# The end of a hybrid encoder layer: the last 256 tokens of three w_down blocks computed with tokens on the output's partitions

## The chip, the core and the metric

The kernel runs on one core of a Trainium2 chip. A core has TensorE (PE, matrix products, with weight loads shown as PEld), VectorE (DVE), ScalarE (ACT), GpSimd (POOL), a queue engine (SP) and 16 DMA engines. Data lies in an on-chip memory of 128 partitions; products go to PSUM, eight banks of 128 x 512 float32. The metric is device time in microseconds (us), the median of the runs; lower is better.

## The reference, cut to what matters

One encoder layer on 512 tokens of width 1024, all in float32:

```python
x = x + 0.5 * swiglu(rms_norm(x, ffn1_norm), ...)     # (silu(h @ w_gate) * (h @ w_up)) @ w_down, inner width 2752
h = rms_norm(x, mix_norm); u = h @ w_in
x = x + concat([fourier_mixer(u), gqa_attention(u)]) @ w_out
x = x + 0.5 * swiglu(rms_norm(x, ffn2_norm), ...)
return rms_norm(x, final_norm)                         # x / sqrt(mean(x*x) + 1e-6) * final_norm
```

The change concerns the last two lines: the last part of the second feed-forward's w_down product, its addition to x with the factor 1/2, and the final norm.

## The kernel before, in words

**Layout.** x lies transposed: feature on the partition (eight blocks `x[0]` to `x[7]` of 128 features), token on the free axis. Every operand of a float32 product is split into a high and a low part, and `product` (lines 153 to 156) does three TensorE products, high x high, high x low and low x high, into one PSUM accumulation. Each has its own weight load of 128 columns from the stationary operand, while the moving operand streams 256 or 512 columns.

**Memory.** Tiles come from pools that are laid one behind the other in each partition: `const` (with `ring`, twelve slots of 4 KB that hold the split weights, then `gx` with gains and x, then small ones: sums, means, powers), `weights` (three raw tiles, tag `raw`), `temps`, and behind these a region used by stage: in a feed-forward `at` (split activations, the moving operand of w_down), `rt` (split inputs of the seven-product scheme) and `sums` (raw gate and up weights `raw_g`, `s`, `raw_u`). The function `room` (line 87) leaves a gap; `room(cp, 192)` stands behind `ring`, and two of 192 bytes ahead of `at` and of `rt` (lines 257 and 259). A small tile takes a multiple of 32 bytes. In the program as built `ring` starts at byte 8320 of a partition, `at` at 110464 and `rt` at 139328; in the mixing stage a tile `more` of further weights starts at 110464 as well.

**Feed-forward.** The inner width is done in four groups. The first group's gate and up products are plain; the others go through `seven` (line 411): Winograd-like, seven half-size products in place of eight. Its `multiply` (line 422) issues all of them at line 429:

```python
nc.tensor.matmul(
    ps[:, c], a[:, ks], b[:, i, c], start=first and i == 0 and o == 0,
```

with `a` a 128-column piece of a `ring` slot as weights and `b[:, i, c]` 256 columns of `rt` as the moving operand (in the first product of a group two of them are cut into 64 and 192 columns). After each group comes w_down, for the eight output blocks d = 0 to 7: `down` (line 560) converts a block's weights into two slots (line 146 the high part on ScalarE, line 117 the low part on VectorE), and its steps stream 512 columns of `at`. `residual` (line 580) adds half the PSUM bank to `x[d]`. Raw weights are loaded some blocks ahead, by SP (line 132).

**Order.** Feed-forward runs in the order in which it is written on PE and SP; from the second group on ScalarE and VectorE follow it too. GpSimd is left to the scheduler. The mixing stage follows a written list.

**The end.** In the last group (seven column blocks of the inner width) w_down runs in full for d = 0 to 4. For d = 5, 6, 7 `closing` (line 1402) first does tokens 0 to 255 (`t0`), 21 products of 256 columns a block, each followed by residual (VectorE), square (ScalarE), addition of the squares (line 1409) and multiplication by the final gain in place (`gained`, line 1393). Then it does the same for tokens 256 to 511 (`t1`); between those products PE sums the squares of the first 256 tokens over the partitions (line 209, a product with a column of ones), 1/rms goes through VectorE and GpSimd (`mean`, line 216, and `power`, line 223), is turned into a row by transposes (line 228) and `finish` (line 1377) multiplies and stores the first 256 tokens. Behind the last product the same chain runs for tokens 256 to 511, with `awake` products (line 1400) as fillers, and nine stores in all go to one output tensor `out_y`, feature on the partition; the host transposes it.

Of the kernel before, what the change touches and what calls it, by code (L numbers as in the profile page):

```python
# [6 lines left out]
F32 = mybir.dt.float32  # L7
# [6 lines left out]
P = 128  # L14
# [16 lines left out]
USES = "a11", "s1", "a12", "s2", "s4", "s3", "a22"  # L31
KH = KD // 2
HEAD = 64
HI_DVE = ("f0", "f1")
SWAP_DMA = ("q1", "q2", "q3")

# [38 lines left out]
def asf(ap):  # L75
    return ap.bitcast(F32)
# [3 lines left out]
def encoder(ctx, tc, A, out):  # L80
# [17 lines left out]
    def bank(name):  # L98
        return pp.tile([P, S], F32, tag="bank", name=name)
# [58 lines left out]
    class Norm:  # L158
# [71 lines left out]
        def row(self, c0=0, c1=4):  # L230
# [4 lines left out]
            t = slice(c0 * P, c1 * P)  # L235
            nc.scalar.copy(self.rb[:, t], ps[:, t])
            return ps

        def rows(self, c0, c1):

            pss = [bank(f"rp{self.n}_{c0}{i}") for i in range(2)]
            for ps in pss:
                for c in range(c0, c1):
                    self.turn(ps, c)
            t = slice(c0 * P, c1 * P)
            nc.scalar.copy(self.rb[:, t], pss[1][:, t])
            return pss[0]

    def ffn(norm, after, wgu, wd, wdt, groups, opening, closing):

# [5 lines left out]
        with tc.tile_pool(name=f"act{n_}", bufs=1) as ap, tc.tile_pool(name=f"sums{n_}", bufs=2) as sp:  # L256
# [329 lines left out]
            for gi, group in enumerate(groups):  # L586
                last = gi == len(groups) - 1
                ahead, waiting, downs = [], [], []

                def more_downs(n):  # L590
                    while len(downs) < min(n, KD):
                        downs.append(down(len(downs), group, gi))

                if gi:
                    with in_full_order():
                        rest = seven(
                            range(group[0] + 1, min(group[-1] + 2, NF)), *ready, lambda i: more_downs(i + 1)
                        )
                else:
                    lent = [at[:, i].rearrange("p a b -> p (a b)") for i in range(PLACES - 4, PLACES)]  # L600
                    plain.extend(lent)
                    row = []
                    pss = dict(enumerate(opening(gate, lambda: norm.column([norm.acc]), lambda: row.append(norm.row()))))
                    back(lent[:2])
                    due, parts, left = [*pss, "t"], list(range(KH)), range(2 * len(pss), 2 * n_plain)
                    pss["t"] = [gate(2 * NF)]
                    tail_weights()
                    for i, c in enumerate(left):
                        pss.setdefault(c // 2, []).append(gate(c, by_dma=i in (1,) if n_ else i > 0))
                        if due:  # L610
                            j = due.pop(0)
                            for _ in evacuate(at[:, place(j)], n_, pss[j], norm):
                                pass
                        if c % 2 and c != left[-1]:
                            due.append(c // 2)
                        while len(parts) * len(left) > (len(left) - 1 - i) * KH:
# [12 lines left out]
                with in_full_order():  # L629
                    for d in range(KD):  # L630
                        if last and closing and d == KD - 3:
                            break
                        if last and d == KD - 2:
                            back(lent)
                        ps = bank(f"dn{n_}_{d}_{gi}")
                        if not last and d in (0, 4):
                            new = Pair(groups[gi + 1][0] + 1 + d // 4)
                            new.load_rest()
                            if d == 0:
                                ready = [new]  # L640
                                ahead.extend(new.steps())
                            else:
                                ready.append(new)
                        steps = downs[d](ps, every)
                        for _ in range(len(group) - (last and d < 2)):
                            next(steps)
                        waiting.append((d, ps, steps))
                        if last and d == 0:
                            rest()
                            lent = slots[KD - 2 : KD]  # L650
                            plain[0:0] = lent
                            more_downs(3)
                            continue
                        for d_, ps, steps in waiting:
                            for _ in steps:
                                pass
                            residual(d_, ps, every)
                        more_downs(d + (3 if gi and not last else 4))
                        if not gi:
                            next(left_over, None)  # L660
                        elif d == 0:
                            rest()
                        for d_, *_ in waiting:
                            added(d_)
                        waiting = []
                if last and closing:
                    closing([(e, down(e, group, gi) if e >= len(downs) else downs[e]) for e in range(KD - 3, KD)], residual)
                if not gi:
                    back(lent)
                free.extend(where[j] for j in group)  # L670
# [706 lines left out]
    def finish(c0, c1, row, parts):  # L1377
# [3 lines left out]
        for ks in parts:  # L1381
# [5 lines left out]
                y = xt[:, block, t]  # L1387
                nc.vector.tensor_tensor(out=y, in0=y, in1=pr[:, t].unsqueeze(1).to_broadcast(list(y.shape)), op=ALU.mult)
            queue = nc.scalar if ks[0] in by_pool else nc.sync
            queue.dma_start(out=out[:, block, t], in_=xt[:, block, t])  # L1390

    def gained(k, t=slice(0, S)):
        nc.scalar.activation(x[k][:, t], x[k][:, t], AF.Copy, scale=gains[:, 3, k : k + 1])

    def awake(n):

        unit = ident.bitcast(BF16)
        ps = bank("awake")
        for _ in range(2 * n):
            nc.tensor.matmul(ps[:, : 2 * P], unit[:, :P], unit, start=True, stop=True)  # L1400

    def closing(downs, residual):

        for k in range(downs[0][0]):
            gained(k)
        t0, t1 = slice(0, S // 2), slice(S // 2, S)

        def more(sq, t):
            nc.vector.tensor_tensor(out=n3.acc[:, t], in0=n3.acc[:, t], in1=sq[:, t], op=ALU.add)

        for d, steps in downs:
            ps = bank(f"last{d}0")
            for _ in steps(ps, t0):
                pass
            residual(d, ps, t0)
            more(n3.square(d, t0), t0)
            gained(d, t0)
        i = 0
        for d, steps in downs:
            ps = bank(f"last{d}1")  # L1420
            for _ in steps(ps, t1):
                i += 1
                if i == 5:
                    n3.column([n3.acc], 0, 2)
                if i == 9:
                    finish(0, 2, n3.row, ((0, 1), (4, 5), (2, 3), (6, 7)))
            if d < KD - 1:
                residual(d, ps, t1)
                sq = n3.square(d, t1)
                if d == downs[0][0]:  # L1430
                    more(sq, t1)
                gained(d, t1)

        pc = bank("ss3_2")
        for c in (2, 3):
            n3.sum(pc, c, [n3.acc], first=c == 2, last=False, skip_group_check=True)
        awake(1)
        for c in (2, 3):
            n3.sum(pc, c, [sq], first=False, last=False, skip_group_check=True)
        residual(KD - 1, ps, t1)  # L1440
        sq = n3.square(KD - 1, t1)
        gained(KD - 1, t1)
        for c in (2, 3):
            n3.sum(pc, c, [sq], first=False, last=c == 3, skip_group_check=True)
        awake(2)
        n3.mean(pc, 2, 4)
        n3.power(2, 4)
        finish(2, 4, n3.rows, ((0,), (1,), (4, 5), (2, 3), (6, 7)))

    with in_order():  # L1450
        ffn(n2, n3, A["wgu2"], A["wd2"], A["wdt2"], GROUPS2, lambda gate, column, row: [[gate(0, {KD - 1: column}), gate(1, {3: row})]], closing)


def _order():
# [37 lines left out]
def _layout(i):  # L1492
# [13 lines left out]
    def down(w):  # L1506
# [29 lines left out]
        "wins": chunks(w_in[:, np.concatenate([k, q, v])]),  # L1536
        "winf": w_in[:, :512].reshape(2, 4, P, 2, 256).transpose(3, 0, 2, 1, 4).reshape(4, P, 4, 256),
        "wo": chunks(i["w_out"][mix]),
    }


# [19 lines left out]
```

## Time and profile before

| what | us |
|---|---|
| median of the runs | 843.41 |
| profiled execution | 843.26 |
| its span, first to last instruction | 841.0 |
| PE busy | 833.3 (99%) |
| PE weight loads busy | 754.4 (90%) |
| DVE busy | 606.1 (72%) |
| ACT busy | 463.5 (55%) |
| POOL busy | 63.5 (8%) |

"Busy" counts overlapping products once, so a busy PE says only that a product was under way. The chain that ended last follows the work back from the last instruction to what released it at each step. A group row gives line, engine, operation, output <- inputs, shape and count, then busy us, mean ns of one, and the idle time ahead of it. A window row gives the window, its length, then busy us and instructions of PE, PEld, DVE, ACT and POOL, the granted clock of PE, the busy share of the DMA engines and GB/s. In the chain and the timeline the first number is the start in us, the second the length.

### The profile page before, as it was taken

To read this page: it belongs to the slowest core of one execution; us is meant where nothing else is said; L and a number is where in the kernel's file an instruction comes from. 1 tells how busy PE (TensorE), PEld (TensorE's weight loads), DVE (VectorE), ACT (ScalarE), POOL (GpSimd) and SP (SyncE) were. 2 spreads that over 40 slices of the span, in tenths; PEclk is the share of its full clock that TensorE was granted. 3 is DMA by queue.
4 is the path that set the end of the run, shared out by engine and by line. 5 is a ranking of instruction groups with operands and counts; after the bars stand their busy time and mean duration, and the time that the engine had idled before them with its cause. 6 is when DMAs were issued, how large, how long until landed. Compare 5 with 4: busy or idle time off the path is not lost.

```text
span 841.0 us, 13697 instructions
## 1 busy us (share of the span) xinstructions
PE 833.3 (99%) x5440; PEld 754.4 (90%) x5440; DVE 606.1 (72%) x927; ACT 463.5 (55%) x771; POOL 63.5 (8%) x70
## 2 busy tenths in 40 slices
PE   9999999999999999999999999999999999999996
PEld 6888998899989998889988888899988998899986
DVE  6987884578557867699998478788755884578563
ACT  7753663366435644677776346456533663366452
POOL 0121000000000000222000000110000100000002
PEclk9999999999999999999999999999999999999998
DMA  7796774467365423414020325778563674556123
GB/s 250 188 225 163 195 188 142 123 164 215 104 161 148 122 60 110 150 51 139 27 74 26 98 57 146 190 191 211 161 175 101 177 206 134 121 160 184 45 66 100
DMA packets 46382, 116.76 MB, mean 139 GB/s; under 512 B 5232, under 2 KB 10864, under 8 KB 46192
## 3 DMA queue, kind: packets, MB, share of 16 engines
q1 hardware_dynamic: 38240, 92.05, 33.2%
q0 software_dynamic: 7536, 23.34, 16.7%
q8 instruction: 42, 0.69, 0.3%
q10 hardware_dynamic: 544, 0.52, 0.2%
q14 instruction: 20, 0.16, 0.1%
HBM read 111.44 MB, written 2.10 MB: 135 GB/s over the span
## 4 chain that ended last, share of the span: by engine, by line
PE 94%; DVE 3%; DMA 1%; issue 1%; ACT 0%; POOL 0%; POOLq 0%; SPq 0%; ACTq 0%
PE r L429 23%; PE q L429 11%; PE dn L156 8%; PE dn L154 8%; PE dn L155 8%; PE p L429 6%; PE mix L154 4%; PE mix L156 3%; PE mix L155 3%; PE gu L762 3%; PE mix L1252 2%; PE mix L1209 2%; PE gu L154 1%; PE gu L155 1%; PE gu L156 1%; DMA raw_dn<-in_wd 1%
## 5 line engine op out<-in xcount | busy, mean ns | idle before, releaser
L429 PE MATMUL r<-rt,ring 128*128 128x256 f32 x1686 | 204.9, 276 | 0.0
L429 PEld LDWEIGHTS r<-rt,ring 128*128 128x128 f32 x1686 | 198.5, 188 | 0.9
L155 PE MATMUL dn<-at,ring 128*128 128x512 f32 x295 | 114.8, 389 | 0.0
L156 PE MATMUL dn<-at,ring 128*128 128x512 f32 x295 | 114.8, 389 | 0.0
L154 PE MATMUL dn<-at,ring 128*128 128x512 f32 x295 | 114.8, 389 | 0.0
L429 PE MATMUL q<-rt,ring 128*128 128x256 f32 x840 | 106.6, 276 | 0.0
L374 ACT CAST ring<-s 128x1024 fp32r<-128x1024 f32 x70 | 73.5, 1050 | 58.0 <-DVE s L394 53.0
L581 DVE SCALAR_TENSOR_TENSOR gx<-dn,gx 128x512 f32<-128x512 f32 x61 | 42.1, 691 | 81.7 <-PE dn L156 81.7
L429 PEld LDWEIGHTS q<-rt,ring 128*128 128x128 f32 x840 | 100.4, 188 | 0.0
L146 ACT CAST ring<-raw_dn 128x768 fp32r<-128x768 f32 (+2 forms) x51 | 43.6, 858 | 80.4 <-PE dn L155 76.8
L117 DVE TENSOR_TENSOR ring<-s,ring 128x1024 fp32r<-128x1024 f32 x70 | 85.3, 1218 | 0.6 <-ACT ring L374 0.6
L156 PEld LDWEIGHTS dn<-at,ring 128*128 128x128 f32 x295 | 55.4, 188 | 11.5
L155 PEld LDWEIGHTS dn<-at,ring 128*128 128x128 f32 x295 | 55.4, 188 | 11.1
L154 PEld LDWEIGHTS dn<-at,ring 128*128 128x128 f32 x295 | 55.4, 188 | 11.0
L346 POOL DMA_DIRECT2D s<-in_wgu x35 | 30.1, 861 | 427.2 <-DMA s<-in_wgu 171.1
L117 DVE TENSOR_TENSOR ring<-raw_dn,ring 128x768 fp32r<-128x768 f32 (+2 forms) x51 | 50.0, 984 | 5.8 <-ACT ring L146 5.5
L429 PE MATMUL p<-rt,ring 128*128 128x256 f32 x420 | 53.3, 276 | 0.0
L429 PEld LDWEIGHTS p<-rt,ring 128*128 128x128 f32 x420 | 50.2, 188 | 0.0
L117 DVE TENSOR_TENSOR ring<-raw_g,ring 128x1024 fp32r<-128x1024 f32 x35 | 42.6, 1217 | 0.0
L117 DVE TENSOR_TENSOR at<-u,at 128x512 fp32r<-128x512 f32 x35 | 24.2, 693 | 20.3 <-ACT at L484 20.2
L472 DVE TENSOR_TENSOR u<-g,u 128x512 f32<-128x512 f32 x35 | 24.0, 686 | 19.8 <-ACT u L469 19.8
L374 ACT CAST ring<-raw_g 128x1024 fp32r<-128x1024 f32 x35 | 36.8, 1051 | 0.0
(308 smaller groups left out, 1551.3 us busy)
## 6 DMA issues: line engine op xcount, KB each, us to landing
s<-in_wgu SPq DMA_DIRECT2D x70, 256.0 KB, 4.3
s<-in_wgu POOLq DMA_DIRECT2D x35, 512.0 KB, 5.6
raw_g<-in_wgu SPq DMA_DIRECT2D x35, 512.0 KB, 4.2
raw_dn<-in_wd SPq DMA_DIRECT2D x44, 384.0 KB, 3.9
raw_u<-in_wgu SPq DMA_DIRECT2D x35, 256.0 KB, 4.5
raw_gu<-in_wgu SPq DMA_DIRECT2D x12, 512.0 KB, 3.5
raw_o<-in_wo SPq DMA_DIRECT2D x8, 512.0 KB, 3.5
raw_dn<-in_wd SPq DMA_DIRECT2D x8, 448.0 KB, 4.0
```

Of the source, the lines that this page charges most:

```text
L117: nc.vector.tensor_tensor(out=lo, in0=src, in1=asf(hi), op=ALU.subtract)
L146: nc.scalar.copy(hi[:, :n, :], raw[:, :n, :])
L154: nc.tensor.matmul(ps, whi, mhi, start=first, stop=False)
L155: nc.tensor.matmul(ps, whi, mlo, start=False, stop=False)
L156: nc.tensor.matmul(ps, wlo, mhi, start=False, stop=last)
L346: nc.gpsimd.dma_start(out=blocks(t), in_=up, accum_op=ALU.add)
L374: nc.scalar.copy(ts[0], src)
L429: nc.tensor.matmul(ps[:, c], a[:, ks], b[:, i, c], start=first and i == 0 and o == 0, stop=i == KH - 1 and o == 2, skip_group_check=not fi ...
L472: nc.vector.tensor_tensor(out=self["u"], in0=self["g"], in1=self["u"], op=ALU.mult)
L581: nc.vector.scalar_tensor_tensor(out=x[d][:, t], in0=ps[:, t], scalar=0.5, in1=x[d][:, t], op0=ALU.mult, op1=ALU.add)
L762: nc.tensor.matmul(pss[c], w[:, k % 2, c], m[k], start=k == 0 and m is hh and w is hi, stop=k == KD - 1 and w is lo,)
L1209: nc.tensor.transpose(pts[n][:, c * P : (c + 1) * P], prob[t, b, c][:, kc * P : (kc + 1) * P], ident)
```

## The change

Blocks 5, 6 and 7 of the last group keep the old way for tokens 0 to 255. For tokens 256 to 511, in two chunks of 128, the roles are exchanged: the activations (128 tokens) are the stationary operand, and the weights of all three blocks, 384 columns, the moving one, so the product comes out with tokens on the partitions. Its PSUM bank (`high`) is started with transposes of x[4] to x[7] for that chunk; the products are accumulated on the last 384 columns. To this end the three blocks' weights are halved in the conversion and lie side by side in six slots (0 to 2 the high parts, 3 to 5 the low ones), 64 bytes into them. x[0] to x[3], already multiplied by the gain, are transposed into a second bank (`low`). The squares of the 384 columns are summed along the free axis by ScalarE into a [128,1] tile (`ssend2`, `ssend3`, both new in the `const` pool) and added to the mean that the other five blocks gave; 1/rms is then a number per partition, and ScalarE and VectorE scale `low` and `high` into `y`, which takes a raw weights' place. The final gains of the upper four blocks come as a new input `fg` of 128 x 512. The output is two tensors: the first 256 tokens as before, the last 256 with tokens on the partition. `Norm.rows`, `awake` and `closing` go.

In the program as built every engine has the same instructions in the same order as before up to the conversion of block 5's weights. `at` now starts at byte 110528, `rt` at 139392, `more` at 110528; `ring` stays at 8320.

```diff
+    class Ending:
+        def __init__(self, at, where, js, wd):
...
+            self.w = [
+                ring[:, a : a + 3].rearrange("p s c -> p (s c)")[:, 16 : 16 + len(js) * ENDS * P].rearrange(
+                    "p (j d c) -> p j d c", d=ENDS, c=P
+                )
+                for a in (0, 3)
+            ]
+        def weights(self, d):
+            n, js = len(self.js), self.js
+            raw = raw_tile(self.wd[d][:, js[0] : js[-1] + 1, :], f"end{d}", n)[:, :n]
+            hi, lo = (w[:, :, d - self.first] for w in self.w)
+            nc.scalar.activation(hi, raw, AF.Copy, scale=0.5)
+            nc.vector.scalar_tensor_tensor(out=lo, in0=raw, scalar=0.5, in1=asf(hi), op0=ALU.mult, op1=ALU.subtract)
...
+        def by_columns(self, d, t):
+            ps = bank(f"last{d}0")
+            for i, j in enumerate(self.js):
+                whi, wlo = (w[:, i, d - self.first] for w in self.w)
+                product(ps[:, t], whi, wlo, *self.acts(j, t), i == 0, i == len(self.js) - 1)
...
+        def by_tokens(self, c, between={}):
+            t = slice(c * P, (c + 1) * P)
+            low, high = bank(f"low{c}"), bank(f"high{c}")
+            self.turned(high, range(KH, KD), t)
+            whi, wlo = (w.rearrange("p j d c -> p j (d c)") for w in self.w)
+            ps = high[:, S - ENDS * P :]
+            for i, j in enumerate(self.js):
+                between.get(i, int)()
+                if i == 3:
+                    self.turned(low, range(KH), t)
+                h, l = self.acts(j, t)
+                for a, w in ((h, whi), (h, wlo), (l, whi)):
+                    nc.tensor.matmul(
+                        ps, a, w[:, i], start=False, stop=i == len(self.js) - 1 and a is l, skip_group_check=True
+                    )
+            sq = tp.tile([P, S], F32, tag="sq", name=f"sqend{c}")
+            ss = cp.tile([P, 1], F32, name=f"ssend{c}")
+            nc.scalar.activation(sq[:, : ENDS * P], ps, AF.Square, scale=D**-0.5, accum_out=ss)
+            r = n3.r[:, c : c + 1]
+            ms = n3.ms[:, c : c + 1]
+            nc.vector.tensor_tensor(out=ms, in0=ms, in1=ss, op=ALU.add)
+            n3.power(c, c + 1)
+            y = wp.tile([P, D], F32, tag="raw", name=f"y{c}")
+            nc.scalar.activation(y[:, :S], low, AF.Copy, scale=r)
+            nc.vector.scalar_tensor_tensor(out=y[:, S:], in0=high, scalar=r, in1=self.gain, op0=ALU.mult, op1=ALU.mult)
+            for h in range(2):
+                cs = slice(h * S, (h + 1) * S)
+                nc.sync.dma_start(out=out[1][(c - 2) * P : (c - 1) * P, cs], in_=y[:, cs])
+        def run(self):
+            self.gain = tp.tile([P, S], F32, tag="g", name="gain")
+            nc.sync.dma_start(out=self.gain, in_=A["fg"])
...
+            for d in range(self.first, KD):
+                self.by_columns(d, t)
+                if d == self.first:
+                    for c in (2, 3):
+                        n3.sum(pc, c, [n3.acc], first=c == 2, last=c == 3, skip_group_check=True)
+                    n3.mean(pc, 2, 4)
+            self.by_tokens(2, {
+                2: lambda: n3.column([n3.acc], 0, 2),
+                6: lambda: finish(0, 2, n3.row, ((0, 1), (4, 5), (2, 3), (6, 7))),
+            })
+            self.by_tokens(3)
```

`by_columns` goes on with residual, square, addition and gain for its block as before, `turned` issues one transpose per block into a bank, and `more_downs` calls `ending.weights(d)` for d = 5, 6, 7.

More of the change, by code (lines that the diff above doesn't have):

```diff
@@ L33 @@
 HEAD = 64
+ENDS = 3
 HI_DVE = ("f0", "f1")
@@ L237, in row @@
             return ps
[L239 to L247, printed above, removed]
     def ffn(norm, after, wgu, wd, wdt, groups, opening, closing):
@@ L588, in ffn @@
                 ahead, waiting, downs = [], [], []
+                ending = closing(at, where, list(group), wd) if last and closing else None
                 def more_downs(n):
                     while len(downs) < min(n, KD):
-                        downs.append(down(len(downs), group, gi))
+                        d = len(downs)
+                        downs.append(ending.weights(d) if ending and d >= KD - ENDS else down(d, group, gi))
                 if gi:
@@ L630, in ffn @@
                     for d in range(KD):
-                        if last and closing and d == KD - 3:
+                        if ending and d == KD - ENDS:
                             break
@@ L665, in ffn @@
                         waiting = []
-                if last and closing:
-                    closing([(e, down(e, group, gi) if e >= len(downs) else downs[e]) for e in range(KD - 3, KD)], residual)
+                if ending:
+                    more_downs(KD)
+                    ending.run()
                 if not gi:
@@ L1389, in finish @@
             queue = nc.scalar if ks[0] in by_pool else nc.sync
-            queue.dma_start(out=out[:, block, t], in_=xt[:, block, t])
+            queue.dma_start(out=out[0][:, block, t], in_=xt[:, block, t])
     def gained(k, t=slice(0, S)):
         nc.scalar.activation(x[k][:, t], x[k][:, t], AF.Copy, scale=gains[:, 3, k : k + 1])
[L1395 to L1448, printed above, removed]
@@ new lines, in encoder, with acts, turned @@
+    class Ending:
+        def __init__(self, at, where, js, wd):
+            self.at, self.where, self.js, self.wd = at, where, js, wd
+            self.first = KD - ENDS
+            self.w = [
[10 more added lines that the diff above has]
+            nc.vector.scalar_tensor_tensor(out=lo, in0=raw, scalar=0.5, in1=asf(hi), op0=ALU.mult, op1=ALU.subtract)
+        def acts(self, j, t):
+            return (self.at[:, self.where[j], o, t] for o in range(2))
+        def by_columns(self, d, t):
[3 more added lines that the diff above has]
+                product(ps[:, t], whi, wlo, *self.acts(j, t), i == 0, i == len(self.js) - 1)
+            nc.vector.tensor_tensor(out=x[d][:, t], in0=ps[:, t], in1=x[d][:, t], op=ALU.add)
+            sq = n3.square(d, t)
+            nc.vector.tensor_tensor(out=n3.acc[:, t], in0=n3.acc[:, t], in1=sq[:, t], op=ALU.add)
+            gained(d, t)
+        def turned(self, ps, ks, t):
+            for i, k in enumerate(ks):
+                nc.tensor.matmul(
+                    ps[:, i * P : (i + 1) * P], x[k][:, t], ident, start=i == 0, stop=i == len(ks) - 1,
+                    is_transpose=True, skip_group_check=True,
+                )
[11 more added lines that the diff above has]
+                for a, w in ((h, whi), (h, wlo), (l, whi)):
+                    nc.tensor.matmul(
+                        ps, a, w[:, i], start=False, stop=i == len(self.js) - 1 and a is l, skip_group_check=True
+                    )
+            sq = tp.tile([P, S], F32, tag="sq", name=f"sqend{c}")
[14 more added lines that the diff above has]
+            nc.sync.dma_start(out=self.gain, in_=A["fg"])
+            for k in range(KH):
+                gained(k)
+            t = slice(0, 2 * P)
+            gained(KH, t)
+            pc = bank("ss3_2")
+            for d in range(self.first, KD):
[9 more added lines that the diff above has]
+            self.by_tokens(3)
@@ L1450, in encoder @@
     with in_order():
-        ffn(n2, n3, A["wgu2"], A["wd2"], A["wdt2"], GROUPS2, lambda gate, column, row: [[gate(0, {KD - 1: column}), gate(1, {3: row})]], closing)
+        ffn(n2, n3, A["wgu2"], A["wd2"], A["wdt2"], GROUPS2, lambda gate, column, row: [[gate(0, {KD - 1: column}), gate(1, {3: row})]], Ending)
 def _order():
@@ L1538, in _layout @@
         "wo": chunks(i["w_out"][mix]),
+        "fg": np.broadcast_to(i["final_norm"][KH * P :], (P, S)),
     }
@@ L1553 @@
     }
-    out = nc.dram_tensor("out_y", (P, KD, S), F32, kind="ExternalOutput").ap()
+    out = [
+        nc.dram_tensor(f"out_{n}", shape, F32, kind="ExternalOutput").ap()
+        for n, shape in (("cols", (P, KD, S // 2)), ("rows", (S // 2, D)))
+    ]
     with tile.TileContext(nc, schedule_with_timeline_sim=True) as tc:
@@ L1557 @@
     r = run_bass_kernel_spmd(nc, [{f"in_{n}": a for n, a in arrays.items()}], core_ids=[0])
-    y = np.asarray(r.results[0]["out_y"])
-    y = y.transpose(1, 0, 2).reshape(1, D, S).transpose(0, 2, 1)
+    cols, rows = (np.asarray(r.results[0][f"out_{n}"]) for n in ("cols", "rows"))
+    y = np.concatenate([cols.transpose(2, 1, 0).reshape(S // 2, D), rows])[None]
     return np.ascontiguousarray(y[:, np.argsort(_order())])
```

## The prediction

> **What bounds the kernel now.** I read the page first, then the chain that ended last, then short timelines.
>
> ```profile
> span 841.0 us, 13697 instructions
> PE 833.3 (99%) x5440; PEld 754.4 (90%) x5440; DVE 606.1 (72%) x927; ACT 463.5 (55%) x771; POOL 63.5 (8%) x70
> PE 94%; DVE 3%; DMA 1%; issue 1%; ACT 0%; POOL 0%; POOLq 0%; SPq 0%; ACTq 0%
> L429 PE MATMUL r<-rt,ring 128*128 128x256 f32 x1686 | 204.9, 276 | 0.0
> L429 PE MATMUL q<-rt,ring 128*128 128x256 f32 x840 | 106.6, 276 | 0.0
> L429 PE MATMUL p<-rt,ring 128*128 128x256 f32 x420 | 53.3, 276 | 0.0
> L156 PE MATMUL dn<-at,ring 128*128 128x512 f32 x295 | 114.8, 389 | 0.0
> ```
>
> TensorE is the bound: 94% of the chain, with no idle time ahead of its large groups. The largest is line 429, the seven-product scheme: 1686 + 840 + 420 = 2946 products; 12 of them are the narrower pieces of the first product of each of six groups, which leaves 2934 of 256 columns. Inside it nothing else is near the bound:
>
> ```profile
> 742.00:752.00 10.00, 10.00 (x90) 10.00 (x90) 8.29 (x13) 5.83 (x11) 0.00 (x0) 1.00 0.71 184
> ```
>
> Here PE and its weight loads are busy for all 10 us, VectorE for 8.3, ScalarE for 5.8, at full clock. A change of nanoseconds per product in this stage goes straight into the time. So I compared the spacing of products. First the chain, with start and length of each piece: 24 products of line 429, and 512-wide ones of w_down.
>
> ```profile
> 751.52 2.72 PE r L429 x24
> ...
> 801.90 0.23 PE dn L154
> 802.13 0.23 PE dn L155
> ...
> 810.74 0.23 PE dn L154
> ```
>
> Then the 256-wide products elsewhere: the window of the first half of the end (63 `last` products; two neighbours count in its x65), and the timeline in the middle of the kernel.
>
> ```profile
> 816.02:823.58 7.56, 7.56 (x65) 7.55 (x64) 4.09 (x7) 4.13 (x7) 0.00 (x0) 1.00 0.01 2
> ```
> ```profile
> 403.15 0.28 PE L1058 MATMUL mix<-ring 128*128 128x256 f32 x1
> 403.27 0.28 PE L1059 MATMUL mix<-ring 128*128 128x256 f32 x1
> 403.39 0.28 PE L1060 MATMUL mix<-ring 128*128 128x256 f32 x1
> ```
>
> Line 429 issues a 256-wide product every 2.72/24 = 113.3 ns. The end needs 7.56/63 = 120.0 ns for products of the same width, type and accumulation, and so does the projection in the middle (120 ns from row to row). The 512-wide ones are (810.74 - 801.90)/39 = 226.7 apart. Something makes line 429 6.7 ns faster, and the kernel's layout has one difference: where the moving operand lies against the stationary one. In the program as built, `ring`, which holds the weights, starts at byte 8320 of a partition (a multiple of 128) and all its pieces are multiples of 512 further on. `at` starts at 110464, also a multiple of 128; `rt` at 139328, 64 bytes past one. In the middle both operands lie in `ring`. So where both operands are in step modulo 128 bytes the spacing is 120, and where they are 64 apart it is 113.3.
>
> **The change part by part.**
>
> *The shift.* Up to the last group's third w_down block the built program has the same instructions in the same order on every engine, so one might cost everything before the end at nothing. But `ssend2` and `ssend3`, two [128,1] tiles in the `const` pool, take 32 bytes each, and everything allocated behind that pool moves by 64: `rt` to 139392, a multiple of 128; `at` to 110528, 64 past one. `ring` stays. Line 429 is now in step, the case that this trace shows at 120.0. Its cost: 2934 x (120.0 - 113.3) ns = 19.6 us, the upper bound. Nearest row below: just after an interruption in-step products start closer together, as in the first ones of the end:
>
> ```profile
> 816.02 0.28 PE L154 MATMUL last<-at,ring 128*128 128x256 f32 x1
> 816.13 0.28 PE L155 MATMUL last<-at,ring 128*128 128x256 f32 x1
> 816.25 0.28 PE L156 MATMUL last<-at,ring 128*128 128x256 f32 x1
> 816.37 0.28 PE L154 MATMUL last<-at,ring 128*128 128x256 f32 x1
> ```
>
> 0.11, then 0.12. Line 429 runs for hundreds of products without interruption, so I take nearly all: **+19.3**; lower bound nothing, if the layout isn't the reason. Nothing hides it, since PE has no idle time there.
>
> ```profile
> L1059 PE MATMUL mix<-more,ring 128*128 128x256 f32 x16 | 4.5, 282 | 0.0
> ```
>
> The other way round, this group and its neighbours of lines 1058 and 1060, 48 products whose moving operand lies in `more`, get faster by 6.7 ns, since `more` moves out of step with `ring`: **-0.3**.
>
> The 512-wide products also change step, by `at`. I take no change. The first `last` product above follows a 512-wide one, its operands are in step, a weight load runs beside it, and it still took 0.11: streaming 256 columns in step is possible in about 113 ns, so 512 at 227 is twice that, and what is slow at 256 is the weight load, for which 512 columns leave time. VectorE's conversions don't care for the step:
>
> ```profile
> L117 DVE TENSOR_TENSOR ring<-s,ring 128x1024 fp32r<-128x1024 f32 x70 | 85.3, 1218 | 0.6 <-ACT ring L374 0.6
> L117 DVE TENSOR_TENSOR ring<-raw_gu,ring 128x1024 fp32r<-128x1024 f32 x6 | 7.3, 1220 | 1.3 <-ACT ring L146 1.2
> ```
>
> `s` is 64 off `ring`, `raw_gu` in step: 1218 and 1220 ns.
>
> *The end on TensorE.* The timeline of before, and a group of transposes elsewhere in it:
>
> ```profile
> 401.92 1.04 PE L1209 MATMUL mix<-ident,e 128*128 128x128 f32 x8
> 402.72 0.36 PE L1058 MATMUL mix<-ring 128*128 128x256 f32 x1
> 402.92 0.28 PE L1059 MATMUL mix<-ring 128*128 128x256 f32 x1
> ...
> 817.98 0.69 DVE L193 TENSOR_TENSOR acc<-acc,sq 128x512 f32<-128x512 f32 x1
> ...
> 823.78 0.42 DVE L581 SCALAR_TENSOR_TENSOR gx<-last,gx 128x256 f32<-128x256 f32 x1 [1.19 <-PE last L156]
> 824.23 0.42 ACT L187 ACTIVATE sq<-gx 128x256 f32<-128x256 f32 x1 [1.56 <-DVE gx L581]
> 824.68 0.42 DVE L1409 TENSOR_TENSOR acc<-acc,sq 128x256 f32<-128x256 f32 x1 [0.48 <-ACT sq L187]
> ...
> 831.65 0.28 PE L156 MATMUL last<-at,ring 128*128 128x256 f32 x1
> 831.77 0.51 PE L209 MATMUL ss<-ones,acc 128*128 128x2 f32 x4
> ```
>
> From 816.02 to 831.77 are 15.75 us: 126 products at 0.120 are 15.12, and one pair of column sums and two turns of r the other 0.63, of which I give the sums two thirds, 0.42. After: 63 products stay, 7.56. The other 63 become 42 of 384 columns, at 384/256 of 113.3 or of 120 ns, 0.170 to 0.180 each; I take 0.172, 7.2 in place of 7.56: -0.34. Sixteen transposes come in four groups: in the rows eight take 0.80 and the product behind them 0.20 in place of 0.12, so a group of four is 0.44, four of them +1.76. The sums over tokens 256 to 511 come ahead of the last product: +0.42, and a wait. They need block 4's squares added, which VectorE had at 818.67 and now has 0.1 later (the last weights' low part becomes a scalar_tensor_tensor), while PE arrives at 816.02 + 21 x 0.12 = 818.54: +0.3. Together the last product starts 2.15 later, near 833.8, and its result is there at 834.15 (before: 831.93).
>
> Of the other waits put into PE's order, the sums over tokens 0 to 255 need residual, square and addition of the last block, 1.5 us by the three rows at 823.78; PE has a group of transposes and six products before them, 0.44 + 1.03. No cost, or a tenth. Their r has the following 2.4 us.
>
> *Behind the last product.* The timeline, then rows of grouped instructions, then of the DMA issues:
>
> ```profile
> 833.55 0.16 DVE L216 TENSOR_SCALAR ms<-ss 128x2 f32<-128x2 f32 x1 [1.15 <-PE ss L209]
> 833.78 0.70 POOL L223 TENSOR_TENSOR r<-ms,mhalf 128x2 f32<-128x2 f32 x1 [4.22 <-DVE ms L216]
> ...
> 837.12 0.39 ACTq L1390 DMA_DIRECT2D out_y<-gx  x1
> ```
> ```profile
> L1197 ACT ACTIVATION_READ_ACCUMULATOR e<-mix,mx,sc 128x1 f32 x32 | 6.3, 196 | 0.0
> ...
> L882 ACT ACTIVATE sq_q<-mix 128x512 f32<-128x512 f32 x4 | 2.4, 591 | 0.0
> ```
> ```profile
> L912 DVE SCALAR_TENSOR_TENSOR rot_q<-mix,qkg,cos 128x512 f32<-128x512 f32 x1 | 0.7, 749 | 0.4 <-ACT sw_q L895 0.4
> ```
> ```profile
> out_y<-gx SPq DMA_DIRECT2D x5, 256.0 KB, 2.4
> ...
> out_y<-gx ACTq DMA_DIRECT2D x2, 256.0 KB, 3.0
> ```
>
> Before, 5.2 us pass from the last product's result to the last issue at 837.12. Now: square of 384 columns out of PSUM 0.48 (from 0.591 for 512) and its accumulator 0.20, an addition 0.16, the power 0.70, then the two halves of y side by side, 0.75 on VectorE, with 0.05 between steps: 2.5, to 836.7. SP issues two transfers 0.39 apart, the last at 837.1: the same time as before. But 512 KB are on their way then, not 1 MB, since tokens 256 to 383 have left 4 us earlier, beside products. So the last transfer lands in 2.4 or a little less and not in 3.0: the end comes out **-0.5**. Bounds: -2 (transposes at the 0.06 that a quarter of a 512-wide product takes, no wait for VectorE) and +2 (products at 0.180, a microsecond more of waiting, landing in 3.0).
>
> Costed at nothing: the halved weights, 0.1 longer on VectorE per block under 4.8 us of products (21 x 0.227), into slots that are free since the last seven-product is over; without that cover 0.3. The gains' transfer on SP has nothing behind it until the first store.
>
> *The sum* is made against the profiled execution's 843.26 (span 841.0 and 2.3 around it), 0.15 below the median of 843.41: 843.26 + 19.3 - 0.3 - 0.5 = **861.8**.
>
> A rule speaks against this. The Trainium skill, "TensorE: Matmul & The Clock Gate", section "Step-by-step: what each phase is for", has two independent read ports, one for weights and one for the moving operand, so that loading the next weights doesn't take read bandwidth from the running product. By it the shift of 64 bytes costs nothing. The rows disagree with it so far: 113.3 and 120.0 ns for products that differ only in the step.
>
> Its section "PE-mode transpose" gives about 275 ns for a 128x128 transpose in a kernel. As an estimate by that page, sixteen would add 4.4 rather than 1.76. The trace has the 0.10 per transpose used above.
>
> **The rivals.**
>
> 1. *Not slower: the spacing has another cause than the addresses.* The seven-product stage writes other banks and runs beside more VectorE work than the end; if one of these sets the 6.7 ns, nothing before the end changes and the time is 843.26 - 0.5 = **842.8**. Against it: three groups in step, in two stages, all show 120, and busier neighbours should not make products faster. 11%.
> 2. *The 512-wide products gain what line 429 loses.* If being in step costs any product 6.7 ns, the 885 of w_down (3 lines x 295) come down from 226.7 to 220: 5.9 less, **855.9**, or 854 with the other 512-wide groups that change step. For it: 226.7 - 120.0 is 106.7, a clean rate. Against it: the 0.11 in step above. 13%.
> 3. *The end stalls*, on VectorE or on PSUM: its place is the accumulation of products on transposes in one bank, which no row shows. At 3 us or more, **865** and up. 6%.
>
> That the change doesn't do what it says is excluded by the built order of instructions, short of the results' values.
>
> **How the numbers follow.** The forecast, 861.8, has 70%; its own spread is about 860 to 864.5 (the end's bounds, and 18.5 to 19.6 for line 429). The range takes in rival 2, down to 853.5, and stops at 864.5; 842.8 and the long stall stay out. 2%, 17 us, is about what a measurement of this kernel can tell from no change, and 860.3 is that line: the forecast lies 1.5 above it, so a twentieth of its chance, rival 2 and rival 1 make 0.28 for within 2%; slower by more 0.71; faster 0.01.
>
> **What the profile after would show.** Chain pieces of 24 products of line 429 of 2.88 in place of 2.72, and their mean 283 in place of 276 (that is what `last` has now); w_down 512-wide unchanged at 0.227; about 19 us of the difference before the end begins; four groups of transposes of 0.44; from the last product's start to the span's end 6.7 in place of 9.4. I am wrong if line 429 stays at 2.72, or if w_down's spacing falls to 0.220.

## The result and the profile after

The kernel after takes **867.72 us** (median; 867.35 to 868.48) against 843.19 for the kernel before, measured beside it: 1.0294 times as long, 95% interval 1.0282 to 1.0306. It is slower, by 24.5 us, where 18.5 were forecast. One of the four executions of the kernel before took 2174.77 us, and the ratio leaves it out. The profiled execution took 867.68, its span is 865.5.

The page of the kernel after, engines and largest groups:

```profile
span 865.5 us, 13644 instructions
PE 858.7 (99%) x5417; PEld 773.8 (89%) x5417; DVE 603.9 (70%) x923; ACT 462.0 (53%) x770; POOL 62.5 (7%) x69
L420 PE MATMUL r<-rt,ring 128*128 128x256 f32 x1686 | 215.5, 283 | 0.0
L156 PE MATMUL dn<-at,ring 128*128 128x512 f32 x295 | 117.2, 397 | 0.0
L420 PE MATMUL q<-rt,ring 128*128 128x256 f32 x840 | 112.2, 283 | 0.0
```

TensorE still fills 99% of the span and nothing idles ahead of the large groups, but the mean of a seven-product multiplication (line 429 before, line 420 now) went from 276 to 283 ns, and that of a w_down product from 389 to 397. The second was to stay. The chain of the kernel after gives the spacing, 24 products of line 420, then 30 products of w_down of which the first and the last are shown:

```profile
763.84 2.88 PE r L420 x24
...
834.62 0.23 PE dn L155
...
841.39 0.23 PE dn L157
```

2.88/24 is 120.0 ns (113.3 before). (841.39 - 834.62)/29 is 233.4 ns (226.7 before). So *both* widths lost 6.7 ns, at most 2934 x 6.67 = 19.6 us for line 420 and 885 x 6.67 = 5.9 us for w_down. The timeline of the end:

```profile
841.45 0.27 PE L155 MATMUL last<-at,ring 128*128 128x256 f32 x1
...
849.59 0.60 PE L1426 MATMUL high<-ident,gx 128*128 128x128 f32 x4
849.94 1.29 PE L1444 MATMUL high<-ring,at 128*128 128x384 f32 x6
851.18 0.61 PE L210 MATMUL ss<-ones,acc 128*128 128x2 f32 x4
851.64 0.78 PE L1444 MATMUL high<-ring,at 128*128 128x384 f32 x3
...
857.42 2.33 PE L1444 MATMUL high<-ring,at 128*128 128x384 f32 x12
...
860.64 0.55 POOL L224 TENSOR_TENSOR r<-ms,mhalf 128x1 f32<-128x1 f32 x1 [2.95 <-DVE ms L1452]
861.23 0.75 DVE L1456 SCALAR_TENSOR_TENSOR y<-high,r,gain 128x512 f32<-128x512 f32 x1 [0.67 <-POOL r L224]
```

The end's first `last` product starts at 841.45, before at 816.02: 25.4 us are lost by then. Summed from each product's start to the next one's, in both traces, line 420 has 19.0 of them and w_down 5.6. Another 0.7 lie in the 120 gate and up products whose weights are a part of `at` (about 227 ns apart before, 233 after). Line 420 stays below 19.6 chiefly because 72 of its 2934 products stand between products of w_down; these were at 117.7 before and are at about 119.8 now. From there to the span's end it is 24.05 against 24.98: the new end is 0.9 us shorter.

### The profile page after: what moved, and what is told of

It is laid out like the page before. It is cut to its first block, busy times and chain, and to the rows that moved or that the text cites. A ratio compares the mean times of both kernels' runs of the same rounds, so it can differ in the third digit from the quotient of the medians.

```text
span 865.5 us, 13644 instructions
## 1 busy us (share of the span) xinstructions
PE 858.7 (99%) x5417; PEld 773.8 (89%) x5417; DVE 603.9 (70%) x923; ACT 462.0 (53%) x770; POOL 62.5 (7%) x69
## 4 chain that ended last, share of the span: by engine, by line
PE 98%; DVE 0%; issue 0%; ACT 0%; POOLq 0%; POOL 0%
PE r L420 23%; PE q L420 12%; PE dn L157 8%; PE dn L155 8%; PE dn L156 8%; PE p L420 6%; PE mix L155 3%; PE mix L156 3%; PE mix L157 3%; PE gu L757 3%; PE gu L155 3%; PE gu L156 3%; PE gu L157 3%; PE mix L1247 2%; PE mix L1204 2%; PE mix L1053 1%
## 5 line engine op out<-in xcount | busy, mean ns | idle before, releaser
L420 PE MATMUL r<-rt,ring 128*128 128x256 f32 x1686 | 215.5, 283 | 0.0
L420 PEld LDWEIGHTS r<-rt,ring 128*128 128x128 f32 x1686 | 208.9, 192 | 1.0
L156 PE MATMUL dn<-at,ring 128*128 128x512 f32 x295 | 117.2, 397 | 0.0
L155 PE MATMUL dn<-at,ring 128*128 128x512 f32 x295 | 117.1, 397 | 0.0
L157 PE MATMUL dn<-at,ring 128*128 128x512 f32 x295 | 117.1, 397 | 0.0
L420 PE MATMUL q<-rt,ring 128*128 128x256 f32 x840 | 112.2, 283 | 0.0
L420 PEld LDWEIGHTS q<-rt,ring 128*128 128x128 f32 x840 | 105.8, 192 | 0.0
L147 ACT CAST ring<-raw_dn 128x768 fp32r<-128x768 f32 (+2 forms) x48 | 40.6, 850 | 77.1 <-PE dn L156 73.7
L420 PE MATMUL p<-rt,ring 128*128 128x256 f32 x420 | 56.1, 283 | 0.0
L420 PEld LDWEIGHTS p<-rt,ring 128*128 128x128 f32 x420 | 52.9, 192 | 0.0
L118 DVE TENSOR_TENSOR ring<-raw_dn,ring 128x768 fp32r<-128x768 f32 (+2 forms) x48 | 46.7, 976 | 8.0 <-ACT ring L147 7.9
L452 DVE TENSOR_TENSOR g<-p,p 128x256 f32<-128x256 f32 x35 | 14.8, 424 | 39.1 <-PE p L420 39.1
```

What stands on the lines that cost most here:

```text
L118: nc.vector.tensor_tensor(out=lo, in0=src, in1=asf(hi), op=ALU.subtract)
L147: nc.scalar.copy(hi[:, :n, :], raw[:, :n, :])
L155: nc.tensor.matmul(ps, whi, mhi, start=first, stop=False)
L156: nc.tensor.matmul(ps, whi, mlo, start=False, stop=False)
L157: nc.tensor.matmul(ps, wlo, mhi, start=False, stop=last)
L420: nc.tensor.matmul(ps[:, c], a[:, ks], b[:, i, c], start=first and i == 0 and o == 0, stop=i == KH - 1 and o == 2, skip_group_check=not fi ...
```

## The experiments

All distances below are those of the moving operand from the stationary one, modulo 512 bytes. For line 420 that is `rt` against `ring`, for w_down `at` against `ring`. Before: `at` 256, `rt` 448. After: `at` 320, `rt` 0. The gaps (`room`) ahead of `at` and of `rt` set them freely.

**Before's addresses under the kernel after.**

```diff
-            room(ap, 192)
+            room(ap, 128)
             at = ap.tile([P, PLACES, 2, S], F32R, name=f"at{n_}")
```

> The changed kernel with the gap ahead of `at` cut from 192 to 128 bytes, so that `at` and `rt` lie where they lay before the change (110464 and 139328); the new end is kept. Theory addresses: line 420 goes from 120.0 back to 113.3 ns per product (19.5 us) and the 512-wide w_down products from 233.3 back to 226.7 (885 of them, 5.9 us), so 867.7 - 25.4 = about 842.3; against the kernel before what is left is the new end alone, about 1 us faster. Rival, the new end or its order slows what is ahead of it: stays near 867.

Measured: 842.87 against 843.08, ratio 0.9999, interval 0.9991 to 1.0008. The whole loss is gone, with the new end, its waits, its output and its tiles all in place. The microsecond that the new end was to gain doesn't show in the median. The page and the chain, a piece of the second group and one of the fourth:

```profile
L156 PE MATMUL dn<-at,ring 128*128 128x512 f32 x295 | 114.9, 389 | 0.0
L420 PE MATMUL r<-rt,ring 128*128 128x256 f32 x1686 | 206.1, 277 | 0.0
```
```profile
182.83 2.72 PE r L420 x24
...
572.32 2.83 PE r L420 x24
```

w_down is back at 389. Line 420 is at 113.3 in five of its six groups (three in each feed-forward); in the fourth it is at 2.83/24 = 117.9, with operands at the same distance. The fourth group costs 2.2 us by that (489 products x 4.4 ns). Two of the eleven executions, this profiled one (844.19) and another (844.74), lie 1.3 and 1.9 us above the median; for the second there is no trace to say whether it is the same.

**The shift alone**, under the kernel before: two tiles of 32 bytes that nothing uses.

```diff
     n3 = Norm(3)
+    for c in (2, 3):
+        nc.vector.memset(cp.tile([P, 1], F32, name=f"ssend{c}"), 0.0)
```

> The kernel before with two more [128,1] tiles in the const pool and nothing else (two memsets of 0.06 us): every tile behind the pool moves by 64 bytes as in the change, the end is the old one. Theory addresses: 843.2 + 19.5 + 5.9 and a few tenths = 868 to 869, slower than the changed kernel by the gain of its end (about 1 us). Rival, the change's own instructions cost the time: 843.

Measured: 868.84, ratio 1.0305 (1.0291 to 1.0319). So 64 bytes of unused memory make the kernel before as slow as the kernel after, and 1.1 us slower still: that is what the new end saves on these addresses (25.16 us from the first `last` product to the span's end in this trace, 24.09 in that of the kernel after).

**One operand at a time.** First `rt` moved to where it was before, `at` left at 320:

```diff
             at = ap.tile([P, PLACES, 2, S], F32R, name=f"at{n_}")
-            room(ap, 192)
+            room(ap, 128)
             rt = ap.tile([P, 7, 2, KH, HALF], F32R, name=f"rt{n_}")
```

> The changed kernel with the gap ahead of `rt` cut to 128 bytes: `rt` lies as before the change, `at` stays 64 bytes further up. Theory addresses, each operand by itself: line 420 at 113.3, w_down at 233.3, so about 867.7 - 19.5 = 848.2. Rival, the two are coupled (one bank pattern for the stage): another time, 842 or 867.

Measured: 854.00, ratio 1.0130 (1.0115 to 1.0146), span 851.6. The chain, a piece each of the first, the second and the fourth group:

```profile
98.80 2.72 PE r L420 x24
...
184.26 2.83 PE r L420 x24
...
577.82 2.72 PE r L420 x24
```

The first and the fourth group run at 113.3, the other four at 117.8, though `rt` lies where it was before. All six follow a w_down stage with `at` at 320. But ahead of the first and the fourth it is that of a plain group, whose last products have their weights in `at` as well, or in a tile that moved along, so that their distance stays a multiple of 256; they stand 226.7 apart. Ahead of the other four w_down comes to 229.0 ns by the starts in the trace, not to the 233.3 that it has after at the same distance. The time is neither the theory's 848.2 nor one of the rival's two, but the two terms aren't independent.

Then the reverse: `at` back at 256, `rt` left at 0.

```diff
-            room(ap, 192)
+            room(ap, 128)
             at = ap.tile([P, PLACES, 2, S], F32R, name=f"at{n_}")
-            room(ap, 192)
+            room(ap, 256)
             rt = ap.tile([P, 7, 2, KH, HALF], F32R, name=f"rt{n_}")
```

> The kernel after with gaps of 128 and 256 bytes: at 256 bytes from ring modulo 512 as in before, rt at 0 as in after. Theory (256-column products cost 120.0 at a distance that is a multiple of 256, 512-column ones 226.7 there and 6.7 more elsewhere, and the two terms add): w_down back at 226.7, line 420 at 120.0, so 19.6 more than the 839.4 to 840.5 of e10: a span of 859 to 860. Rival, the two terms are one, since w_down's rhythm goes over into the next group: then w_down or line 420 also lands elsewhere, as in e2, and the span is 2 us or more off that.

Measured: 861.51, ratio 1.0219 (1.0201 to 1.0237), span 859.2. The page, and the chain:

```profile
L420 PE MATMUL r<-rt,ring 128*128 128x256 f32 x1686 | 215.5, 283 | 0.0
L156 PE MATMUL dn<-at,ring 128*128 128x512 f32 x295 | 115.0, 390 | 0.0
```
```profile
186.79 2.88 PE r L420 x24
```

This is the case that the prediction described, line 420 at 120.0 and w_down unchanged, and its time lies by the 861.8 forecast for it. What the kernel after has above it, 865.5 - 859.2 = 6.3 us, is mostly `at`: by the starts in the two traces 5.2 in w_down (227.3 to 233.1 on average) and 0.7 in the gate and up products whose weights lie in `at`.

**Both operands elsewhere**, `at` at 448 and `rt` at 64, then `at` at 128 and `rt` at 384:

```diff
-            room(ap, 192)
+            room(ap, 320)
             at = ap.tile([P, PLACES, 2, S], F32R, name=f"at{n_}")
-            room(ap, 192)
+            room(ap, 128)
```

> The changed kernel with `at` 448 and `rt` 64 bytes past `ring` modulo 512 (before: 256 and 448; changed: 320 and 0). Theory parity, only the distance modulo 128 counts: line 420 at 113.3, w_down at 233.3, about 848. Theory direction, the distance modulo 256 counts and 64 ahead isn't 64 behind (the 256-wide products of the middle with their operand in `more` took 118 at 64 ahead): line 420 near 118, w_down unknown, about 860.

```diff
-            room(ap, 192)
+            room(ap, 0)
             at = ap.tile([P, PLACES, 2, S], F32R, name=f"at{n_}")
-            room(ap, 192)
+            room(ap, 256)
```

> The kernel after, with the gap ahead of at 0 and that ahead of rt 256 bytes: at 128 and rt 384 bytes from ring modulo 512, both multiples of 128. If the step modulo 128 decides: line 420 at 120.0 as in the kernel after, w_down back at 226.7, so 5.9 less than the kernel after, a span near 859.6. If the distance modulo 512 or 256 decides, line 420 at 384 may have 113.3 or 117.8 and the span lies between 840 and 853.

Measured: 859.03 with a span of 856.9, and 863.68 with 861.5. With `rt` at 64, line 420 was at 113.3 in the first group and at 117.8 in five; w_down at 448 was at 233.3. That is near the second theory's 860. In the second kernel, the chain in two groups:

```profile
94.06 2.85 PE r L420 x24
...
776.22 2.85 PE r L420 x24
```

118.7 at a distance of 384, and w_down at 128 came to 232.3 to 233.3 by the starts in the trace. Neither of the two numbers expected of this run came out: 128 is not like 0 and 256. The step modulo 128, on which the prediction rested, is not the rule.

**Products alone.** So the distance was swept in a kernel that computes nothing of the layer: 36 products in a row, three for each of four (256 columns) or seven (512) pieces of weights, in the order of the layer's, with all operands zero, on an otherwise idle core at full clock (granted clock 1.00); four such runs at each distance, behind one narrow product of 64, 96, 160 or 224 columns.

```python
for i in range(run // 3):
    ...
    for o, (a, b) in enumerate(((0, 0), (0, 1), (1, 0))):
        at = shift + a * D + k * P
        mv = d + (2 * k + b) * n
        nc.tensor.matmul(ps[:, :n], w[:, at : at + P], m[:, mv : mv + n], ...)
```

> A kernel of products alone (nothing of the layer is computed): runs of 36 products of 256 columns, then of 512, the moving operand 0, 32, ... 480 bytes from the stationary one modulo 512, four runs for each distance, behind one product of 64, 96, 160 or 224 columns. Theory A, the spacing goes by the distance modulo 128: 256 columns 120 ns at 0, 128, 256 and 384 and 113 at 64 and its like; 512 columns 226.7 at 0, 128, 256, 384 and 233.3 at 64 and its like, the same behind each of the four. Theory B, a distance allows several rhythms and the product ahead picks one: at 64 bytes some of the four runs at 113.3 and some at 117.8 for 256 columns, at 229 and at 233 for 512. Theory C, the addresses matter only beside the vector engines' traffic: one spacing for all, since no other engine works here.

Rows of its timeline: one row stands for consecutive products from the start given, so that its length less the last product's 0.28 (256 columns) or 0.39 (512), by the count less one, is the spacing. In order: 256 columns at 0, at 64 behind 64 columns, at 64 behind 96, then 512 columns at 0, 64 and 192.

```profile
30.05 3.88 PE L42 MATMUL bank<-m,w 128*128 128x256 f32 x31
...
65.51 3.11 PE L42 MATMUL bank<-m,w 128*128 128x256 f32 x26
...
69.74 3.22 PE L42 MATMUL bank<-m,w 128*128 128x256 f32 x26
...
311.17 5.83 PE L42 MATMUL bank<-m,w 128*128 128x512 f32 x25
...
378.37 5.89 PE L42 MATMUL bank<-m,w 128*128 128x512 f32 x25
...
514.05 6.00 PE L42 MATMUL bank<-m,w 128*128 128x512 f32 x25
```

These are about 120, 113, 118, 227, 229 and 234 ns, from rounded lengths. Mean spacing of the last 24 products of each run, by their starts in the trace (two values where the four runs differ); 256 to 480 bytes gave the same as 0 to 224:

| distance, bytes | 256 columns, ns | 512 columns, ns |
|---|---|---|
| 0 | 120.0 | 226.7 |
| 32 | 116.7 to 117.8 | 233.3 |
| 64 | 113.3 or 117.8 | 228.9 |
| 96 | 120.0 | 233.3 |
| 128 | 118.6 to 120.0 | 232.1 to 233.3 |
| 160 | 117.2 to 118.7 | 234.2 to 234.5 |
| 192 | 113.3 or 117.8 | 233.3 |
| 224 | 118.3 | 233.3 |

With the weights themselves moved by 64 bytes it was again the difference that counted: 120.0 and 226.7 with both operands moved, 113.3 or 117.8 and 233.3 with the weights alone. So it needs no traffic of the vector engines (theory C falls), the period is 256 and not 128 (A falls), and at 64 and 192 two spacings exist (B holds for 256 columns; the 512-column runs at 64 showed only one, while w_down in the layer showed 229.0 and 233.3 there). Which one a run takes depends on what goes ahead of it, but not on the narrow product's width alone: 113.3 came behind 64 columns at 64 and 192, and behind 96 and 224 columns with the weights moved. The run ahead and the PSUM banks changed along with it and weren't separated. The two widths want opposite things: 512 columns are fastest at 0, where 256 columns are slowest (with 96). Before's layout has `at` at 256, so 0, and `rt` at 448, so 192: the best of these distances for both, as long as line 420 takes the faster of its two spacings.

**How a group is entered.** In the layer the second product of each seven-product group is cut in two (`HEAD`). Two versions of the kernel after, with before's addresses and another cut each, and the kernel before with another cut (the first one's edit is shown, without the gap):

```diff
-HEAD = 64
+HEAD = 128
```

> The kernel after with before's addresses (gap of 128 bytes ahead of at), and the second product of each seven-product group cut into 128 and 128 columns in place of 64 and 192. Theory: which of the two rhythms, 113.3 or 117.8 ns, a group has at 448 bytes from ring is decided by how it is entered, so the cut changes the set of slow groups; the span is 839.9 plus 2.2 for each group of six at 117.8 (1.8 for the third), 840 to 853, with nothing else changed. Rival: the fourth group's 117.8 comes from what the mixing stage leaves behind; then it stays the fourth alone, and the span 842.1.

> As the one before, with the cut at 96 columns. Theory: again another set of slow groups or the same, 839.9 plus 2.2 for each group at 117.8. Rival: the fourth alone, 842.1.

> The kernel before, its cut at 128 columns. Theory: before's six groups are all at 113.3 because of how they are entered, and with another cut some or all go to 117.8: span 841.0 plus 2.2 for each, at most 854. Rival, the addresses alone decide: 841.0 as before.

Measured: 841.79, 842.30 and 843.19, with spans of 839.7, 840.2 and 841.0. All six groups were at 113.3 in all three. With the new end that is the theory's case of no slow group (839.9) and not the rival's 842.1: a fourth group at 117.8 isn't what the mixing stage must leave behind. For the kernel before it is the rival's 841.0: there another cut changed nothing. Whether the cut cures the fourth group, or the profiled execution of the first experiment was an unlucky one, stays open. The first of the three again, with more executions:

> The kernel of e7_head_128 (the kernel after, before's addresses, cut at 128), timed. Theory: the addresses cost nothing and all six groups run at 113.3, so only the new end is left, 1.2 to 1.4 us less: a ratio of 0.998 to 0.999, near 841.9. Rival: a group's rhythm changes from one execution to the next; then single times lie 2.2 apart and the median is within 1 us of before's.

Measured: 842.69 (841.31 to 843.28) against 842.91 (841.91 to 843.78), ratio 0.9995, interval 0.9986 to 1.0004. The median is the rival's, not the theory's 841.9; the spread doesn't speak for the rival, since the kernel before has nearly the same. The profiled execution was one of the three shortest (841.50, span 839.4): all six groups were at 113.3, and from the first `last` product on it took 23.9 us, against 25.0 in the kernel before. Eight of the eleven were 1.0 to 1.8 us longer than that, and no trace says where. Over all executions 0.2 us are left of the new end's gain, within the interval. The kernel equals the kernel before and isn't shown to beat it.

## Why the prediction was wrong

*What bounds the kernel, and where the loss would come from* was right. TensorE's spacing sets the time, and the two small tiles, not the new end, move it: the shift alone gives 1.0305, taking it back 0.9999. Rival 1, that the spacing has another cause than the addresses, is out. The Trainium skill, "TensorE: Matmul & The Clock Gate", section "Step-by-step: what each phase is for", says that loading the next weights takes no read bandwidth from the running product. The runs do not agree with that for every address: with an idle core, the same products take 113.3 or 120.0 ns by 64 bytes of distance.

*Line 420, +19.3.* Right: 120.0 ns, and 19.0 us by the starts in the two traces; the 19.6 of the bound counts the 72 products between those of w_down as if they had been at 113.3. The kernel with `rt` alone moved confirms the size (span 859.2 against 839.4 to 840.2 for those with its end and all six groups at 113.3: 19.0 to 19.8).

*The 512-wide products: "I take no change".* This is the step that failed. It cost +5.6 in w_down and +0.7 in the products that read `at` as weights, and it puts the time outside the range. Its argument was that streaming 256 columns in step took 0.11 once, so that only the weight load is slowed by being in step, and 512 columns leave time for that. In step they do run at 226.7; but out of step they don't stay there, they go to 229 to 234. Nothing in the trace of before showed a long run of 512-wide products out of step, so the term needed a bound on both sides. It had one on one side only, by rival 2, which had them gain: 855.9. The other side, 885 x 6.7 ns = 5.9 us of loss, was never written down, and it is what happened. From trace to trace the sum is 19.0 + 5.6 + 0.7 + 0.1 for the rest - 0.9 for the end = 24.5. The kernel with `rt` alone moved shows the same from the other end: with this term at nothing, 861.5 us.

*"In step modulo 128".* A wrong rule that gave a right number: 0 and 256 were the only multiples of 128 that the trace had in long stages. The period is 256.

*`more`, -0.3.* Smaller. These 48 products went from 119.3 to 117.8 by the starts in the trace, -0.1, and the 512-wide ones that read `more` as weights lost 0.2 (228.5 to 233.3, 48 of them): nothing in sum.

*The end, -0.5.* The sign was right, -0.9 in this profile. On TensorE its parts came out near. Four transposes take 0.35 (849.59 to 849.94) and the product behind them 0.26 in place of 0.17, so a group costs 0.44, as forecast. The Trainium skill, "TensorE: Matmul & The Clock Gate", section "PE-mode transpose", gives about 275 ns for one in a kernel. One lasts 270 to 273 ns in this trace, which agrees, but they start 0.11 apart; the estimate of 4.4 for all sixteen took the length for what each adds. The products of 384 columns are 0.173 to 0.185 apart in place of 0.172. The sums over tokens 256 to 511 met no wait (0.3 forecast), those over tokens 0 to 255 waited 0.1, as forecast. The last product starts at 859.42 (of the twelve from 857.42 on the first two are 0.26 apart, the others 0.173), which is 18.0 behind the first and 2.3 later than before (2.15 forecast). Behind it 6.1 in place of 6.7: 2.6 to the end of the two halves of y (861.98; 2.9 forecast), and 3.6 for the last transfers (3.8). Rival 3, a stall there, didn't come.

## What to carry to other kernels

When a kernel is bound by TensorE, check where its moving operand lies against its stationary one, modulo 256 bytes: here 256-column products were fastest at 64 or 192 and slowest at 0 and 96, and 512-column products fastest at 0. A small tile allocated in an early pool moves every operand behind it; keep a spare gap to put them back, and compare the spacing of products in the untouched stages before judging the part that was changed. Where a known mechanism shifts one of two like terms, bound the other from both sides too.

## What the runs showed that was not expected

The time that two products stand apart depends on the addresses of their operands with nothing else running, in steps of about 6.7 ns: 113.3 and 120.0 ns for 256 columns, 226.7 and 233.3 for 512. Between them lie stable mixed rhythms, 117.8 and 228.9, made of unequal neighbours (117, 118 and 119; 226, 229 and 232) whose mean stays the same for hundreds of products. Such a rhythm, once entered, lasted for a whole group of 489 products; in the sweep it differed at the same distance with what went ahead. Why the two widths prefer opposite distances, and what in the chip has the period of 256 bytes, no run here shows.
